# Top-k's copy to PSUM on VectorE instead of ScalarE, and an earlier hand-over of the low halves in U

## The chip, the cores and the metric

One core of a Trainium2 chip runs the whole program. Its engines are TensorE (PE in the profile, with its weight loads as PEld), VectorE (DVE), ScalarE (ACT), GpSimd (POOL) and SyncE (SP, which here only starts transfers). The metric is the device time of one execution in microseconds; lower is better.

## The reference

Two layers work on 272 rows (256 tokens and 16 meta rows) of width 1024. Each layer mixes tokens (a gated recurrence in layer 0, a convolution in layer 1), normalises, and then runs a feed-forward block that picks experts, which is where most of the time goes:

```python
q = (xc @ w_query).reshape(c, PEER_HEADS, 2, PEER_HALF)
scores = jnp.einsum('chpk,pnk->chpn', q, sub_keys.astype(q.dtype))
s1, i1 = lax.top_k(scores[:, :, 0], PEER_TOPK)
s2, i2 = lax.top_k(scores[:, :, 1], PEER_TOPK)
cand = (s1[..., :, None] + s2[..., None, :]).reshape(c, PEER_HEADS, PEER_TOPK * PEER_TOPK)
s, flat = lax.top_k(cand, PEER_TOPK)
...
expert = idx1 * PEER_N_KEYS + idx2
g = jax.nn.softmax(s.astype(jnp.float32), axis=-1).astype(xc.dtype)
act = jax.nn.gelu(jnp.einsum('chkd,cd->chk', expert_u[expert], xc))
return jnp.einsum('chk,chkd->cd', g * act, expert_v[expert])
```

There are 8 heads, 128 keys on each of two axes (so 16384 experts), and 16 experts are kept per row and head.

## The kernel before

The expert block is done mostly densely. For each of 128 tiles of 128 experts the kernel multiplies the tile of `peer_u` with all rows ("U", PE), applies gelu, multiplies with a gate matrix that is zero where an expert was not picked, and multiplies the result with the tile of `peer_v` ("V"). The last rows of a layer are left out of the dense work; for groups of 16 of them ("few") the picked rows of `peer_u` and `peer_v` are fetched by index (GpSimd's indirect transfers, `few_rows`), and DVE makes the dots (`few_mult`, L1147) and the weighted row sums (`few_add`, L1172 and L1174).

`linears` (from L192) runs over the tiles of U. `load_split` fetches a tile `raw` on SP's queue, ACT casts it to `hi` (L161), and DVE or GpSimd takes the low half `lo = raw - hi` (L170). PE then runs three times 8 matmuls for a tile (L198): hi with the high part of x, hi with the low part, lo with the high part. `raw` has four to five buffers, `hi` and `lo` two each in U. `u_store` (L633) is called behind each tile of U's first half (tiles 0 to 63): it sets the gelu on ACT (L656, `act_a`) and strews the other work between the tiles, by tile numbers at the top of the file. Who makes the low half is decided by `LO_FROM`: GpSimd for the tiles before it, DVE from it on.

Before U, PE makes the scores, ACT copies them out of PSUM (L619), and DVE picks the best: `topk_steps` (from L967). For one group of 128 rows this is 16 times five instructions over 128 scores (L976 to L980), then the copy of the second axis' values to PSUM (`pairs`, L985, on ACT), the sums of candidates (L990), eight times five instructions over the 112 candidates (L999 to L1003), the addresses (L1011 to L1022), and the one-hot look-up of the indices (L1030, L1036, L1041). The second group of rows (`c0` > 0) is done first and whole; the first group (`slow`) runs up to L1003 before U's low halves come to DVE, and its eight last steps are taken at the tiles listed in `SLOW`. In layer 0 one group of few rows needs a small top-k of its own (`few_topk`), whose candidate sums (L990, 128x64 and 128x48) read two tiles in SBUF.

The indices of the first finished group go through DRAM to the few rows: `few_spread` at tile `SPREAD`, `few_fetch` four tiles on, both on SP's queue, and `few_ids` on DVE makes addresses of them at tile `LO_FROM` + 1. Near the end of U's first half the softmax of each group (L1054 to L1065, with a tanh on ACT, L1055) and its turn (`topk_out`: three transposes on PE, L1225, copies on ACT, L1229 and L1230, and one subtraction on DVE) are placed at fixed tiles.

The scheduler keeps the program's order on each engine except where `issue_after` pins an instruction behind another, or where it moves one ahead of work that it does not depend on. Each engine takes its instructions in order.

Of the kernel before, what the change touches and what calls it, by code (L numbers as in the profile page):

```python
# [12 lines left out]
AF = mybir.ActivationFunctionType  # L13
# [21 lines left out]
FEW = META  # L35
DENSE_U, DENSE_V = (240, 224), (192, 176)
EARLY, DRAWN = ((240, 256), (240, 224)), ((224, 208, 192), (208, 192, 176))
DOTS_FROM, DOTS, ROWS, AHEAD, LO_FROM = 34, 20, 2, 2, 31
SLOW = (31, 32, 33, 34, 36, 38, 40, 42)
NEAR = 4  # L40
JG = 4
JA = 64
SPREAD = 26
WROW = 256
PIECES = (0, 32, 64, 96, 120, 128)
FULL = (("v", 1024),)
# [20 lines left out]
class Trunk:  # L67
# [514 lines left out]
    def peer(self, layer, n, xs):  # L582
        tc, nc, a = self.tc, self.nc, self.a
# [9 lines left out]
        with tc.tile_pool(name=f"few{layer}", bufs=1) as kp:  # L593
            iT = ip.tile([HK, n // HC, 2, HC, 2], F16, name="iT")
            ghT = ip.tile([HK, n, 2], F16, name="ghT")
            glT = ip.tile([HK, n], F32, name="glT")
            act_a = ap0.tile([P, JA, nu], F32, name="act_a")

            with tc.tile_pool(name=f"top{layer}", bufs=1) as sp:
                q = sp.tile([P, 2 * HEADS, nq], F32, name="q")  # L600
                for b, (t, bias) in enumerate(self.pre_q):
                    nc.scalar.activation(q[:, b, :], t, AF.Identity, bias=bias)
                self.linears([a["w_query"][layer, b] for b in range(2, 2 * HEADS)], xs, nq, FULL,
                             lambda b, ps: nc.vector.tensor_copy(q[:, 2 + b, :], ps), defer=2,
                             ring=(0, 1, 2, 7, 6))
                picked = []
                early, drawn = ([self.few_new(kp, layer, t0) for t0 in g[layer]] for g in (EARLY, DRAWN))
                near = [few for few in early + drawn if few["t0"] < 2 * P]
                dots = [(few, 0, k) for few in early for k in range(TOPK)]
                dots, later = dots[:DOTS], dots[DOTS:]  # L610
                for c0, md in ctiles:
                    sc = sp.tile([P, 2 * HEADS, NK], F32, tag="sc", name="sc", bufs=2)
                    for g in range(4):
                        ps = self.psum("sps", (3, 4)).rearrange("p (a b) -> p a b", a=4)
                        for i in range(4):
                            b = 4 * g + i
                            nc.tensor.matmul(ps[:, i, :], q[:, b, c0:c0 + P], self.sk[:, 2 * layer + b % 2, :],
                                             start=True, stop=True)
                        nc.scalar.activation(sc[:, 4 * g:4 * g + 4, :], ps, AF.Copy)  # L619
                    if c0:  # L620
                        picked.append((c0, md, *self.topk(sp, sc, P, self.bank(7, "pairs"), True)))
                        for few in early:
                            self.few_turn(sp, few, xs)
                        for few in early:
                            if few not in near:
                                self.few_topk(sp, few, q)
                    else:
                        slow = self.topk_steps(sp, sc, P, HEADS, 2, self.bank(7, "pairs"))
                        for _ in range(3 * HEADS):
                            next(slow)  # L630
                        picked.append((c0, md))

                def u_store(j, ps):  # L633
                    self.fifth = True
                    if j in (LO_FROM, SLOW[-1]):
                        with tc.issue_after(self.last_load):
                            self.few_load(*((sp, early[0], "turned") if j == LO_FROM else (kp, early[1], "kept")))
                    behind = [few for few in early if few.get("left")]
                    if j in SLOW:
                        with tc.issue_after(self.dve_lo.ins):  # L640
                            try:
                                next(slow)
                            except StopIteration as end:
                                picked[-1] += end.value
                    elif j > SLOW[-1] and behind:
                        with tc.issue_after(self.dve_lo.ins):
                            for _ in range(min(2, behind[0]["left"])):
                                self.few_picked(behind[0])
                    e, step = divmod(3 * (j - DOTS_FROM), 4)
                    if 0 <= e < DOTS + AHEAD and step < 3:  # L650
                        with tc.issue_after(self.dve_lo.ins), tc.issue_after(self.lo_ins.ins):
                            if e >= AHEAD:
                                self.few_mult(dots[e - AHEAD][0], dots[e - AHEAD][2])
                            if e < DOTS:
                                self.few_rows(sp, *dots[e], AHEAD + 1)
                    last = nc.scalar.activation(act_a[:, j, :], ps, AF.Gelu_apprx_tanh)  # L656
                    i = j - (JA - 6 - 2 * len(picked))
                    t, odd = divmod(i, 2)
                    if 0 <= t < len(picked) and not odd:
                        c0, m, idx, fv = picked[t]  # L660
                        with tc.issue_after(last.ins), tc.issue_after(self.dve_lo.ins):
                            picked[t] = c0, m, idx, self.softmax(sp, fv, P)
                    if j == SPREAD:
                        with tc.issue_after(self.last_load):
                            self.few_spread(nc.sync, near, "pos", picked[0][2])
                    if j == JA - 1:
                        with tc.issue_after(self.last_load):
                            self.few_spread(nc.sync, near, "z", picked[0][3][:, None])
                    if j == SPREAD + 4:
                        with tc.issue_after(self.last_load):  # L670
                            self.few_fetch(nc.sync, near, "pos")
                    at = 0 if j == LO_FROM + 1 else j - SLOW[-1] - 3
                    if j == LO_FROM + 1 or 0 < at < len(near):
                        with tc.issue_after(self.dve_lo.ins):
                            self.few_ids(near[at], near[at]["pos"])
                    if t == len(picked) and not odd:
                        with tc.issue_after(last.ins):
                            for few in early:
                                if few not in near:
                                    self.few_soft(sp, few)  # L680
                    if 0 < t <= len(picked) and not odd:
                        with tc.issue_after(last.ins), tc.issue_after(self.mm.ins):
                            self.topk_out(*picked[t - 1], iT, ghT, glT)
                self.linears([U[j] for j in range(JA)], xs, nu, lambda j: FULL if j >= LO_FROM else (("p", 1024),), u_store)

            with tc.tile_pool(name=f"act1{layer}", bufs=1) as ap1:
# [104 lines left out]
                for e, (few, i, k) in enumerate(ops):  # L791
                    t = e * (NK - JA - 7) // len(ops) + (2 if i and few is second_ else 0)
# [174 lines left out]
    def topk_steps(self, sp, sc, m, H, parts=1, ps=None, beside=False):  # L967
        nc = self.nc
        K = TOPK
        sv = sp.tile([P, H, 2, K], F32, tag=f"sv{H}", name="sv", bufs=1)  # L970
        si = sp.tile([P, H, 2, K], U32, tag=f"si{H}", name="si", bufs=1)
        for b in range(2 * H):
            s = sc[:m, b, :]
            v, i = sv[:m, b // 2, b % 2, :], si[:m, b // 2, b % 2, :]
# [7 lines left out]
        sv1 = sv[:m, :, 1]  # L982
        if ps is not None:
            sv1 = ps[:m, :H * K].rearrange("p (h k) -> p h k", h=H)
            nc.scalar.activation(sv1, sv[:m, :, 1], AF.Copy)  # L985
        cand = sp.tile([P, H, NEAR * K + (K - NEAR) * NEAR], F32, tag=f"cand{H}", name="cand", bufs=1)
        for part, rows, cols in ((cand[:m, :, :NEAR * K], slice(0, NEAR), slice(0, K)),
                                 (cand[:m, :, NEAR * K:], slice(NEAR, K), slice(0, NEAR))):
# [6 lines left out]
        for h in range(H):  # L995
            s = cand[:m, h]
            v, i = fv[:m, h, :], fi[:m, h, :]
# [502 lines left out]
```

## Time and profile before

| | |
|---|---|
| median of 3 runs | 1816.5 us (1814.68 to 1819.98) |
| the profiled execution | 1818.11 us |
| its span, first to last instruction | 1816.3 us |
| mean granted TensorE clock | 0.972 |
| lo (L170): DVE, GpSimd | 492 at 1225 ns, 62 at 2390 ns |
| hi (L161), ACT | 554 at 1059 ns |
| GpSimd's mean for an indirect row load of `peer_u`, `peer_v` | 1341 ns, 1756 ns |

The page gives for each engine its busy time, a row of 40 slices of the span, and groups of equal instructions with their mean; the list of waits says who stood idle in front of which line and what ended it; a timeline gives instructions in order of time, with the idle time before each in brackets. A group on one line can hold several shapes.

### The profile page before, as it was taken

How to read it: one execution, taken by the hardware profiler on the slowest of the kernel's cores; microseconds unless marked ns; L12 is line 12 of the kernel's file. 1: busy time of each engine (PE TensorE's matmuls, PEld its weight loads, DVE VectorE, ACT ScalarE, POOL GpSimd, SP SyncE). 2: the span in 40 equal slices, each digit the busy share in tenths (PEclk: the TensorE clock that was granted, in tenths of full speed). 3: DMA queues.
4: the chain of work that ended last, by engine and by line, in shares of the span. 5: the costliest groups of instructions: out<-in, count | busy, mean ns of one | idle time of the engine just before them, and what ended most of it. 6: DMA issues, size and time to landing. Idle time of an engine off the chain costs nothing. (4 is left out here: it accounts for less than half of the span.)

```text
span 1816.3 us, 35341 instructions
## 1 busy us (share of the span) xinstructions
PE 1704.8 (94%) x13420; PEld 1661.3 (91%) x13420; DVE 1483.7 (82%) x2888; ACT 1000.8 (55%) x1862; POOL 716.0 (39%) x492
## 2 busy tenths in 40 slices
PE   8999389999999999999999993899999999999997
PEld 7899389999999999999989893899999999999997
DVE  7786933989999789998789869338799997899886
ACT  5553144457777555787532541444577765555453
POOL 1101276324454567753000012763243335687520
PEclk9999699999999999999999996899999999999999
DMA  5545257978788899999541462479797888999984
GB/s 198 163 154 150 58 163 247 343 255 290 252 267 271 303 331 361 369 376 330 198 140 47 133 193 58 151 246 332 257 296 267 278 267 319 348 374 370 338 324 166
DMA packets 136059, 453.35 MB, mean 250 GB/s; under 512 B 23632, under 2 KB 24784, under 8 KB 135760
## 3 DMA queue, kind: packets, MB, share of 16 engines
q1 hardware_dynamic: 98256, 326.23, 53.3%
q0 software_dynamic: 37632, 124.85, 19.0%
q8 instruction: 105, 1.72, 0.4%
q14 instruction: 66, 0.54, 0.1%
HBM read 438.15 MB, written 12.87 MB: 248 GB/s over the span
## 5 line engine op out<-in xcount | busy, mean ns | idle before, releaser
L161 ACT ACTIVATE hi<-raw 128x1024 fp32r<-128x1024 f32 x554 | 586.1, 1059 | 519.3 <-PE acc L820 194.4
L170 DVE TENSOR_TENSOR lo<-raw,hi 128x1024 fp32r<-128x1024 f32 x492 | 600.9, 1225 | 213.6 <-ACT hi L161 198.7
L198 PE MATMUL u<-xs,hi 128*128 128x224 f32 (+3 forms) x4544 | 577.6, 279 | 78.1 <-ACT hi L161 77.3
L198 PEld LDWEIGHTS u<-xs,hi 128*128 128x128 f32 x4544 | 546.1, 193 | 80.5 <-ACT hi L161 78.9
L820 PE MATMUL acc<-w,hi 128*128 128x384 f32 (+1 forms) x1952 | 377.7, 335 | 0.0
L1141 POOL DMA_INDIRECT rows<-peer_v,ids x160 | 280.9, 1756 | 240.3 <-DVE few_out L1174 111.3
L820 PEld LDWEIGHTS acc<-w,hi 128*128 128x128 f32 x1952 | 322.9, 190 | 0.0
L198 PE MATMUL u<-xs,lo 128*128 128x224 f32 (+3 forms) x2272 | 308.4, 277 | 1.3 <-DVE lo L170 1.3
L198 PEld LDWEIGHTS u<-xs,lo 128*128 128x128 f32 x2272 | 282.4, 191 | 1.9 <-DVE lo L170 1.9
L824 PE MATMUL acc<-w,lo 128*128 128x192 f32 (+1 forms) x2016 | 264.2, 272 | 6.4 <-DVE turn L1150 4.6
L824 PEld LDWEIGHTS acc<-w,lo 128*128 128x128 f32 x2016 | 260.2, 192 | 9.3 <-DVE lo L170 9.1
L170 POOL TENSOR_TENSOR lo<-raw,hi 128x1024 fp32r<-128x1024 f32 x62 | 148.0, 2390 | 197.1 <-ACT hi L161 122.2
L1174 DVE SCALAR_TENSOR_TENSOR few_out<-rows,act,few_out 128x1024 f32<-128x1024 f32 x150 | 193.1, 1287 | 20.4 <-DMA rows<-peer_v,ids 17.3
L1141 POOL DMA_INDIRECT rows<-u_rows,ids x64 | 85.8, 1341 | 201.2 <-DVE rows L1147 146.9
L1151 POOL DMA_INDIRECT act<-own,turn x96 | 125.7, 1310 | 31.6 <-issue 24.7
L715 ACT ACTIVATE Bl<-AB,glT 128x128 f16<-128x128 f16 x368 | 112.7, 389 | 21.6 <-PE g L731 16.5
L245 PE MATMUL u<-x,raw 128*128 128x272 f32 x480 | 114.7, 399 | 5.2 <-DMA x<-h 5.2
L245 PEld LDWEIGHTS u<-x,raw 128*128 128x128 f32 x480 | 92.9, 194 | 24.7 <-DMA raw<-w_in 5.1
L1147 DVE SCALAR_TENSOR_TENSOR rows<-rows,wide 128x1024 f32<-128x1024 f32 x64 | 78.0, 1219 | 4.7 <-DMA rows<-u_rows,ids 4.7
L409 POOL TENSOR_SCALAR xs<-x,par 128x272 fp32r<-128x272 f32 (+1 forms) x4 | 3.5, 882 | 180.2 <-DVE x L395 180.2
L710 DVE TENSOR_TENSOR AB<-iota,iT 128x2048 f16<-128x2048 f16 x46 | 57.1, 1245 | 0.0
L985 ACT ACTIVATE pairs<-sv 128x128 f32<-128x128 f32 x4 | 1.1, 281 | 89.7 <-DVE sv L979 89.7
(313 smaller groups left out, 1763.4 us busy)
## 6 DMA issues: line engine op xcount, KB each, us to landing
raw<-peer_u SPq DMA_DIRECT2D x256, 512.0 KB
raw<-peer_v SPq DMA_DIRECT2D x248, 512.0 KB
raw<-w_query SPq DMA_DIRECT2D x28, 512.0 KB
raw<-pw SPq DMA_DIRECT2D x22, 512.0 KB
raw<-w_in SPq DMA_DIRECT2D x16, 512.0 KB
own<-own POOLq DMA_DIRECT2D x18, 256.0 KB
raw<-w_out SPq DMA_DIRECT2D x8, 512.0 KB
raw<-peer_v SPq DMA_DIRECT2D x16, 256.0 KB
```

Source lines behind the costliest of these rows:

```text
L161: self.act_hi = nc.scalar.activation(hi, raw, AF.Copy).ins
L170: i = e.tensor_tensor(lo[:, s], raw[:, s], hi[:, s].bitcast(F32), op=OP.subtract)
L198: self.mm = nc.tensor.matmul(ps[:, :n], l[:, k, :], xs(k, r)[:, :n], start=start, stop=stop)
L245: self.mm = self.nc.tensor.matmul(ps[:, :n], raw[:, k, :], x[:, k, :n], start=k == 0, stop=k == NB - 1)
L710: nc.vector.tensor_tensor(AB.rearrange("p x c (a b) -> p (x c) a b", b=2), keys, iT[:, c0 // HC].rearrange("p x c b -> p (x c) b")[:, :, N ...
L715: nc.scalar.activation(Bl[:, c], Bh[:, c], AF.Copy, scale=glT[:, c0 + c:c0 + c + 1])
L820: self.mm = nc.tensor.matmul(acc[b][:, :2 * n].rearrange("p (a t) -> p a t", a=2), hi, w[:, :, :n], start=j == 0, stop=j == NK - JG - 1, s ...
L824: self.mm = nc.tensor.matmul(main[b][:, :n], hi if p_ else lo, w[:, i, :n], start=False, stop=j == NK - 1 and not p_, skip_group_check=True)
L1141: self.last_rows = self.nc.gpsimd.indirect_dma_start(out=t, out_offset=None, in_=table, in_offset=bass.IndirectOffsetOnAxis(ap=few["ids"][ ...
L1147: self.nc.vector.scalar_tensor_tensor(t, t, 1.0, few["x"], op0=OP.mult, op1=OP.mult, accum_out=few["act"][:, k:k + 1])
L1151: self.nc.gpsimd.indirect_dma_start(out=few["act"][:, k:k + 1], out_offset=None, in_=few["table"].rearrange("p j (t o) -> (p j t) o", o=1) ...
L1174: nc.vector.scalar_tensor_tensor(few["out"], t, w, few["out"], op0=OP.mult, op1=OP.add)
```

## The change

The copy to PSUM in `topk_steps` is made by DVE. `LO_FROM` goes from 31 to 27, and the steps of the slow top-k (`SLOW`) and the first dot (`DOTS_FROM`) come four tiles earlier with it. U's first half does 23 dots in place of 20. Of the second few group 5 row sums in place of 2 are made in U's second half, and so three fewer are left for V. The indices are spread at tile 24, not 26. The first softmax is placed at tile 50 and turned at 53 (before: 54 and 56); the second is placed at 54 and turned at 58 (before: 56 and 58).

```diff
-DOTS_FROM, DOTS, ROWS, AHEAD, LO_FROM = 34, 20, 2, 2, 31
-SLOW = (31, 32, 33, 34, 36, 38, 40, 42)
+DOTS_FROM, DOTS, ROWS, AHEAD, LO_FROM = 30, 23, 5, 2, 27
+SLOW = (27, 28, 29, 30, 32, 34, 36, 38)
+SOFT, OUT = {50: 0, 54: 1}, {53: 0, 58: 1}
...
-SPREAD = 26
+SPREAD = 24
...
-                    i = j - (JA - 6 - 2 * len(picked))
-                    t, odd = divmod(i, 2)
-                    if 0 <= t < len(picked) and not odd:
+                    if j in SOFT:
+                        t = SOFT[j]
...
-                    if t == len(picked) and not odd:
+                    if j == max(OUT):
...
-                    if 0 < t <= len(picked) and not odd:
+                    if j in OUT:
                         with tc.issue_after(last.ins), tc.issue_after(self.mm.ins):
-                            self.topk_out(*picked[t - 1], iT, ghT, glT)
+                            self.topk_out(*picked[OUT[j]], iT, ghT, glT)
...
-            nc.scalar.activation(sv1, sv[:m, :, 1], AF.Copy)
+            nc.vector.tensor_copy(sv1, sv[:m, :, 1])
```

Lines of the changed kernel between the new table and `u_store` stand one further down (hi is L162 there, lo L171). The first place is ACT at the start of U in layer 0; `sc` are the scores, `turned` the few rows for the dots, `act_a` a tile's gelu. Before:

```order
L985 ACTIVATE pairs<-sv 128x128
L161 ACTIVATE hi<-raw 128x1024
L1089 ACTIVATE turned<-wide_ps 16x512 x2
L656 ACT_TABLE_LOAD
L656 ACTIVATE act_a<-u 128x240
L161 ACTIVATE hi<-raw 128x1024
L656 ACTIVATE act_a<-u 128x240
L161 ACTIVATE hi<-raw 128x1024
L656 ACTIVATE act_a<-u 128x240
L161 ACTIVATE hi<-raw 128x1024
L656 ACTIVATE act_a<-u 128x240
L985 ACTIVATE pairs<-sv 128x128
```

The same place in the changed kernel:

```order
L620 ACTIVATE sc<-sps 128x512 x4
L162 ACTIVATE hi<-raw 128x1024
L1089 ACTIVATE turned<-wide_ps 16x512 x2
L657 ACT_TABLE_LOAD
L657 ACTIVATE act_a<-u 128x240
L162 ACTIVATE hi<-raw 128x1024
L657 ACTIVATE act_a<-u 128x240
```

Both copies have left ACT's queue, with hi and act_a in the same order as before; on DVE each now stands one or two instructions ahead of the candidate sums (L990).

The second place is GpSimd, from the low halves of U's first half to the second half in layer 0; `rows` are row loads of the few groups. Before:

```order
L170 TENSOR_TENSOR lo<-raw,hi 128x1024 x31
L1141 DMA rows<-u_rows,ids_1618 128x1024 x16
L1141 DMA rows<-u_rows,ids_1624 128x1024 x6
L773 COPY own<-act_a 128x512
L774 DMA own_224_4356<-own 128x512
```

Now:

```order
L171 TENSOR_TENSOR lo<-raw,hi 128x1024 x27
L1141 DMA rows<-u_rows,ids_1618 128x1024 x16
L1141 DMA rows<-u_rows,ids_1624 128x1024 x9
L773 COPY own<-act_a 128x512
L774 DMA own_224_4365<-own 128x512
```

Four low halves have gone to DVE, and three more row loads of the second group stand ahead of the first `own`.

The third place is ACT near the end of U's first half in layer 0, from the tanh of the second softmax (`z`, 128x128) to the copies of its turn (`iT`, `ghT` with 256 columns). Before:

```order
L1055 ACTIVATE z<-z 128x128
L1229 ACTIVATE iT<-tps 128x8x16 x2
L1230 ACTIVATE ghT<-tps 128x128
L161 ACTIVATE hi<-raw 128x1024
L656 ACTIVATE act_a<-u 128x240
L161 ACTIVATE hi<-raw 128x1024
L656 ACTIVATE act_a<-u 128x240
L1055 ACTIVATE z<-z 128x16
L1229 ACTIVATE iT<-tps 128x16x16 x2
L1230 ACTIVATE ghT<-tps 128x256
```

Now:

```order
L1055 ACTIVATE z<-z 128x128
L162 ACTIVATE hi<-raw 128x1024
L657 ACTIVATE act_a<-u 128x240
L162 ACTIVATE hi<-raw 128x1024
L657 ACTIVATE act_a<-u 128x240
L162 ACTIVATE hi<-raw 128x1024
L657 ACTIVATE act_a<-u 128x240
L162 ACTIVATE hi<-raw 128x1024
L657 ACTIVATE act_a<-u 128x240
L1055 ACTIVATE z<-z 128x16
L1229 ACTIVATE iT<-tps 128x16x16 x2
L1230 ACTIVATE ghT<-tps 128x256
```

Between softmax and turn there were two tiles and the first group's turn; now there are four tiles, and the first turn lies further ahead.

## The prediction

> **What bounds the kernel now.** The page comes first: busy shares and the 40 slices (45.4 us each).
>
> ```profile
> PE 1704.8 (94%) x13420; PEld 1661.3 (91%) x13420; DVE 1483.7 (82%) x2888; ACT 1000.8 (55%) x1862; POOL 716.0 (39%) x492
> PE   8999389999999999999999993899999999999997
> PEclk9999699999999999999999996899999999999999
> ```
>
> TensorE (PE) works 94% of the span. It has two holes, slices 4 and 24 (busy 3 tenths), and its granted clock falls only there (6, and 6 and 8). Both lie at the start of a U stage, one per layer. The list of waits names what ended them:
>
> ```profile
> ACT pairs L985 <- DVE sv L979: 89.7, 4, 37.0
> PE u L198 <- ACT hi L161: 77.3, 7, 33.4
> ```
>
> ScalarE (ACT) waited 89.7 us in four waits in front of the copy to PSUM (L985), and PE waited 77.3 us for the cast hi (L161). The timeline of layer 0 shows that one causes the other. First ACT, then PE (the bracket is the idle time before a row and what ended it):
>
> ```profile
> 183.78 0.28 ACT L985 ACTIVATE pairs<-sv 128x128 f32<-128x128 f32 x1 [9.64 <-DVE sv L979]
> 183.99 1.04 ACT L161 ACTIVATE hi<-raw 128x1024 fp32r<-128x1024 f32 x1
> ...
> 231.24 0.28 ACT L985 ACTIVATE pairs<-sv 128x128 f32<-128x128 f32 x1 [37.02 <-DVE sv L979]
> 231.45 1.04 ACT L161 ACTIVATE hi<-raw 128x1024 fp32r<-128x1024 f32 x1
> ```
>
> ```profile
> 173.26 2.03 PE L198 MATMUL u<-xs,hi 128*128 128x240 f32 x16
> 176.03 1.95 PE L198 MATMUL u<-xs,hi 128*128 128x240 f32 x16
> ...
> 185.08 3.77 PE L198 MATMUL u<-xs,hi 128*128 128x240 f32 x16 [6.21 <-ACT hi L161]
> ...
> 232.55 3.57 PE L198 MATMUL u<-xs,hi 128*128 128x240 f32 x16 [33.45 <-ACT hi L161]
> 236.85 1.95 PE L198 MATMUL u<-xs,hi 128*128 128x240 f32 x16
> 238.63 1.07 PE L198 MATMUL u<-xs,lo 128*128 128x240 f32 x8
> 239.53 1.96 PE L198 MATMUL u<-xs,hi 128*128 128x240 f32 x16
> ```
>
> Each row of 16 with hi begins a tile, so U tile 0 starts at 173.26, tile 1 at 176.03, tile 2 at 185.08, tile 6 at 232.55, tile 7 at 236.85. ACT takes its instructions in order. The copy waits until VectorE (DVE) has its 16 pairs of top-k steps, and the cast of the next tile stands behind it. After each hole PE's first 16 matmuls take 3.57 to 3.77 us, not 1.95. Undisturbed, a tile takes 2.68 us (236.85 to 239.53). Layer 1 is the same:
>
> ```profile
> 1087.64 2.03 PE L198 MATMUL u<-xs,hi 128*128 128x224 f32 x16
> ...
> 1090.40 1.95 PE L198 MATMUL u<-xs,hi 128*128 128x224 f32 x16
> ...
> 1099.84 3.76 PE L198 MATMUL u<-xs,hi 128*128 128x224 f32 x16 [6.60 <-ACT hi L161]
> ...
> 1143.29 3.75 PE L198 MATMUL u<-xs,hi 128*128 128x224 f32 x16 [29.48 <-ACT hi L161]
> ...
> 1147.87 1.95 PE L198 MATMUL u<-xs,hi 128*128 128x224 f32 x16
> ```
>
> **The change part by part.** *The copy on DVE.* DVE made the data, so the copy waits for nothing there. A copy to PSUM with twice the elements is the cast L1011 (row below, 416 ns); 0.2 to 0.4 us each, 0.6 us for two, on DVE's chain alone. On ACT, hi of tile 2 stands behind scores and turned rows only, and PE goes on with tile 2 behind tile 1. Tile 7 then starts in layer 0 at 176.03 + 6 × 2.68 = 192.1 and not 236.85: 44.7 us. In layer 1 it starts at 1090.40 + 6 × 2.68 = 1106.5 and not 1147.87: 41.4 us. Together 86.1 us, all on PE's path, the slow-clock tiles included.
>
> Can the others follow at 2.68 us a tile? GpSimd (POOL) makes the low halves of tiles 0 to 26 now:
>
> ```profile
> 194.04 2.40 POOL L170 TENSOR_TENSOR lo<-raw,hi 128x1024 fp32r<-128x1024 f32 x1 [0.63 <-ACT hi L161]
> 240.02 2.41 POOL L170 TENSOR_TENSOR lo<-raw,hi 128x1024 fp32r<-128x1024 f32 x1 [0.29 <-ACT hi L161]
> ```
>
> 2.40 us beside a busy DVE and 2.41 beside a nearly idle one: it fits, with a gap of 0.29 us.
>
> *The low halves from tile 27.* This moves the hand-over from POOL to DVE four tiles forward. In tiles DVE has 27 instead of 31, in time far less: its top-k used to have PE's holes as cover, and they go. DVE's last top-k instructions, and what it did next:
>
> ```profile
> 242.59 0.27 DVE L1003 FIND_INDEX8 fi<-fv,r 128x8 uint32<-128x112 f32 x1
> 299.15 1.23 DVE L170 TENSOR_TENSOR lo<-raw,hi 128x1024 fp32r<-128x1024 f32 x1 [56.30 <-ACT hi L161]
> ...
> 1153.33 0.27 DVE L1003 FIND_INDEX8 fi<-fv,r 128x8 uint32<-128x112 f32 x1
> ```
>
> DVE was done at 242.9 and 1153.6 and then idle for 56.3 us. Tile 27 will start at 176.03 + 26 × 2.68 = 245.7 (layer 1: 1160.1); PE uses its low half 1.78 us later (236.85 to 238.63), and DVE needs 1.23 us to make it. So DVE must be free by 246.3 (1160.6): slack 3.4 and 7.0 us. Against that stands a new collision. In the old holes POOL was idle; now it is busy 2.4 of every 2.68 us:
>
> ```profile
> 195.47 1.05 DVE L990 TENSOR_TENSOR cand<-sv 128x64 f32<-128x64 f32 x1
> ...
> 196.69 0.20 DVE L990 TENSOR_TENSOR cand<-sv 128x48 f32<-128x48 f32 x1
> ...
> 197.66 0.20 DVE L1016 TENSOR_SCALAR far<-fi 128x128 uint32<-128x128 uint32 x1
> ...
> 198.39 0.28 DVE L1021 SCALAR_TENSOR_TENSOR pu<-pu,fi 128x128 uint32<-128x128 uint32 x1
> ```
>
> The 64-wide sum took 1.05 us and ended as POOL's lo of 194.04 ended (196.44); the 48-wide one behind it took 0.20. That is 0.85 us of waiting for POOL. The six address steps from 197.66 to 198.39 ran with POOL idle. Now two sums (layer 0 only) and six steps meet a busy POOL. Bounds: nothing, if all fall into gaps; a whole lo for each, 8 × 2.40 = 19 us and 6 × 2.40 = 14 us. I take half a lo for the first of a bunch, and two or three short steps per gap (they start 0.13 us apart), which is nearest to the one blocked row: the sums 2, the six steps 1.2 + 2 × 2.68 = 6.6, less 1 for their own run: 7 us in layer 0 and 5.5 in layer 1. PE then waits 7 + 0.6 − 3.4 = 4 us in layer 0 (bounds 0 and 16) and 0 in layer 1 (0 and 8).
>
> The Trainium skill, "SBUF — State Buffer", section "Who interferes with whom", says that a VectorE instruction in a 2-port mode or with two SBUF inputs and a GpSimd one that reads SBUF exclude each other for a whole instruction. The row of 1.05 us agrees. By that rule every one of the eight can be blocked, which is the upper bound above; the sum goes by the rows.
>
> The long one-hot steps have one operand in PSUM; the nearest row is the cast to PSUM, which ran unhurt beside POOL's lo in the stretch from 185 to 199 us:
>
> ```profile
> L1011 DVE CAST pairs<-si 128x256 f32<-128x256 uint32 x1 | 0.4, 416 | 0.0
> ```
>
> I cost them at nothing here.
>
> *23 dots and 5 row sums.* Three dots per layer move from U's second half into its first, and three row sums from V into U's second half.
>
> ```profile
> L1174 DVE SCALAR_TENSOR_TENSOR few_out<-rows,act,few_out 128x1024 f32<-128x1024 f32 x150 | 193.1, 1287 | 20.4 <-DMA rows<-peer_v,ids 17.3
> ...
> L1147 DVE SCALAR_TENSOR_TENSOR rows<-rows,wide 128x1024 f32<-128x1024 f32 x64 | 78.0, 1219 | 4.7 <-DMA rows<-u_rows,ids 4.7
> ...
> 300.00:345.00 45.00, 45.00 (x403) 45.00 (x403) 41.93 (x83) 22.34 (x34) 14.81 (x11) 1.00 0.88 315
> 585.00:930.00 345.00, 342.92 (x2359) 336.19 (x2358) 291.63 (x372) 221.02 (x351) 166.75 (x132) 1.00 0.86 311
> ```
>
> (The last two are stretches: length, then busy time of PE, weight loads, DVE, ACT, POOL.) The first half keeps its density: three dots in four tiles behind the hand-over, as in 300 to 345, where PE was busy 45.00 of 45 us with DVE at 41.93. The second half trades 3 × 1.22 for 3 × 1.29 us: nothing. V loses 3.9 us of DVE work per layer where PE is idle for 2.1 of 345 us: 0, at most 2 per layer. Each of these brings its row load on POOL's queue, one for one. On SP's queue the index transfers stand two loads earlier, while their reader on DVE (ids, behind tile 28's low half) comes four tiles earlier, near 249. SP comes to the last of them when load 28 finds a buffer, that is after the low half of tile 23, which starts at 176.03 + 22 × 2.68 = 235. I cost this at nothing, since some 13 us lie between; if the indices were late, DVE would stand in front of them with the low half of tile 29 queued behind.
>
> *First softmax sooner, turns later.* The second transposes waited for DVE's softmax in both layers:
>
> ```profile
> 379.96 0.33 PE L1225 MATMUL tps<-ident,z 128*128 128x128 f32 x1 [1.97 <-DVE z L1065]
> ...
> 1290.50 0.48 PE L1225 MATMUL tps<-ident,z 128*128 128x128 f32 x1 [1.97 <-DVE z L1065]
> 1290.63 3.57 PE L198 MATMUL u<-xs,hi 128*128 128x224 f32 x16
> ...
> 1294.93 1.95 PE L198 MATMUL u<-xs,hi 128*128 128x224 f32 x16
> ```
>
> Now four tiles lie between softmax and turn instead of two, 5.4 us more: both waits go (2 × 1.97), and layer 1's slow tile behind it (1294.93 − 1290.63 = 4.30, not 2.68: 1.6). Together 5.6; at least 0, if the next wait is as long.
>
> The sum: 86.1 + 5.6 − 4 = 87.7 us. The profiled execution took 1818.1 us (its span 1816.3 and 1.8 around it): 1730.4. The median of the runs is 1.6 lower: 1728.8, so **1729 us**.
>
> **The rivals.** (1) *DVE hands over late.* Each of the eight steps waits a whole lo, in both layers: 24 us of waiting instead of 4, 1749 us. For it: the row of 1.05 us, and a slack of only 3.4. Against: 0.85 us is all that was lost in four lo's.
>
> (2) *ACT stops at the next thing.* The second turned rows need the buffer of the first, and so the first's transfer, which now has less time for it; a table load follows, and both stand ahead of hi of tile 3. If a wait there were as long as the first hole (6.2 us and about 2 more for its slow clock, 8 a layer), the time would be 1745. The profile shows no wait at that place, but the transfer always had the copy's wait as cover.
>
> (3) *Slower than before.* If the ordinary top-k instructions (max, find, replace) were also shut out by POOL. Some 300 of them per layer now run beside POOL; if one in ten waited a lo, 30 × 2.68 = 80 us, less the 44.7 + 3.4 that are there to lose, 32 a layer: 1816.5 + 64 = 1880. It decides from 18 blocked instructions a layer on. Against it stands the group of finds from 185 to 199 us, beside four lo's, with a mean of 276 ns where the last one of 242.59, with POOL between two lo's, took 0.27:
>
> ```profile
> L1000 DVE FIND_INDEX8 fi<-fv,cand 128x8 uint32<-128x112 f32 x9 | 2.5, 276 | 0.0
> ```
>
> (4) *Nothing moves*, because hi waits for something else than the copy: 1816. The rows 183.78 and 183.99 speak against it.
>
> **How the numbers follow.** Forecast 0.82, (1) 0.10, (2) 0.05, (3) 0.02, (4) 0.01. The forecast's own range: no collision and 2 us from V per layer, 1721; to half of the upper bounds, 1737. With most of (1) and all of (2): 1721 to 1746. About 0.3% is what a measurement of this kernel can tell from no change; faster by more 0.97, within it 0.01, slower 0.02.
>
> **What would show it.** No row pairs on ACT; PE without a wait for hi near 179 and 200; tile 7 near 192; clock 9 in slices 4 and 24. POOL busy nine tenths from tile 2 to 26. DVE's sums and address steps longer than 0.2 to 0.3 us, ended with POOL's lo; in layer 0 a PE wait of some 4 us for DVE's lo near 250, in layer 1 none. No wait above 1 us before the second transposes. It is wrong if U still has holes over 10 us, or if DVE's lo makes PE wait beyond tile 32.

## The result, and the profile after

The changed kernel takes 1715.46 us, the median of six runs (1714.68 to 1719.34), where the kernel before took 1817.84 (six runs, 1814.68 to 1820.09). The ratio is 0.944, with a 95% interval of 0.9426 to 0.9455. The forecast was 1729 with a range from 1721 to 1746: the direction and the main mechanism, the copy, hold, but 102.4 us were gained where the sum had 87.7, and the time lies below the range.

The page of the changed kernel, the same three lines as before:

```profile
PE 1687.2 (98%) x13420; PEld 1647.0 (96%) x13420; DVE 1498.9 (87%) x2900; ACT 1000.1 (58%) x1858; POOL 685.3 (40%) x484
PE   8999999999999999999999999999999999999997
PEclk9999999999999999999999999999999999999999
```

TensorE (PE) works 98% of the span, both holes are gone, and the granted clock no longer falls in any slice. The start of U in layer 0, on PE, is a tile every 2.69 us from the second on:

```profile
172.85 2.05 PE L199 MATMUL u<-xs,hi 128*128 128x240 f32 x16
...
175.64 1.96 PE L199 MATMUL u<-xs,hi 128*128 128x240 f32 x16
...
178.33 1.96 PE L199 MATMUL u<-xs,hi 128*128 128x240 f32 x16
```

The hand-over of the low halves at tile 27 is the one wait that the prediction placed in U's first half of layer 0. It is there, and shorter than the 4 us foreseen:

```profile
245.66 1.95 PE L199 MATMUL u<-xs,hi 128*128 128x240 f32 x16
248.86 1.17 PE L199 MATMUL u<-xs,lo 128*128 128x240 f32 x8 [1.25 <-DVE lo L171]
```

To see where the 102.6 us of span went (1816.3 to 1713.7), the start of the same matmul is set side by side in the two traces; the last column is how far the changed kernel is ahead there.

| start on PE of | before | after | ahead |
|---|---|---|---|
| U tile 0, layer 0 | 173.26 | 172.85 | 0.41 |
| U tile 7 | 236.85 | 191.80 | 45.05 |
| U tile 26 | 287.95 | 242.97 | 44.98 |
| U tile 28 | 293.33 | 249.87 | 43.46 |
| U tile 56 | 368.65 | 326.06 | 42.59 |
| U's second half (first g) | 402.62 | 356.98 | 45.64 |
| V (first acc) | 592.49 | 544.31 | 48.18 |
| U tile 0, layer 1 | 1087.64 | 1039.82 | 47.82 |
| U tile 7 | 1147.87 | 1058.66 | 89.21 |
| U tile 28 | 1204.15 | 1114.94 | 89.21 |
| U tile 56 | 1279.19 | 1190.83 | 88.36 |
| U's second half | 1314.67 | 1221.62 | 93.05 |
| V | 1499.79 | 1406.11 | 93.68 |
| end of V (first row L1421) | 1797.02 | 1694.39 | 102.63 |

The first half of U gives 45.2 us in each layer (45.64 − 0.41 and 93.05 − 47.82). That is near the forecast. What the prediction left at nothing is the last line: V of layer 1 gives 8.95 us, while V of layer 0 with the work behind it gives nothing (48.18 to 47.82). The second halves give 2.5 and 0.6.

In the trace of before, V of layer 1 has a place that the prediction never showed. On PE:

```profile
1690.45 2.01 PE L824 MATMUL acc<-w,lo 128*128 128x176 f32 x8 [3.50 <-DVE turn L1150]
1692.26 2.62 PE L820 MATMUL acc<-w,hi 128*128 128x352 f32 x8
1694.67 1.84 PE L824 MATMUL acc<-w,lo 128*128 128x176 f32 x8
...
1698.66 1.50 PE L820 MATMUL acc<-w,hi 128*128 128x352 f32 x8
1700.00 1.02 PE L824 MATMUL acc<-w,lo 128*128 128x176 f32 x8
```

PE waited 3.50 us, and the matmuls behind the wait ran slowly: 2.01, 2.62 and 1.84 us, where 1.02, 1.50 and 1.02 are usual, some 2.9 more. The releaser named is a tiny copy on VectorE (DVE), but it only stood last in a line. DVE, and the queue of GpSimd (POOL), at the same time:

```profile
1687.92 1.28 DVE L1174 SCALAR_TENSOR_TENSOR few_out<-rows,act,few_out 128x1024 f32<-128x1024 f32 x1 [4.36 <-DMA rows<-peer_v,ids]
1689.12 0.15 DVE L1150 COPY turn<-ids 128x1 uint32<-128x1 uint32 x1
1689.18 1.22 DVE L170 TENSOR_TENSOR lo<-raw,hi 128x1024 fp32r<-128x1024 f32 x1
```

```profile
1674.69 2.04 POOL L1151 DMA_INDIRECT act<-own,turn  x1 [0.30 <-issue]
1677.03 1.83 POOL L1151 DMA_INDIRECT act<-own,turn  x1 [0.30 <-issue]
1679.16 1.68 POOL L1141 DMA_INDIRECT rows<-peer_v,ids  x1 [0.30 <-DVE w L293]
```

DVE stood 4.36 us before a row sum, with the low half that PE wanted queued behind. Counted from the end of V, where each load meets its sum one for one, the row that it waited for was loaded by the issue of 1679.16, which stood behind two gathers of activations (draws) and landed 8.76 us after it began. The two draws held the queue from 1674.69 on, 4.47 us, about as long as DVE then waited.

### The profile page after: what moved, and what is told of

The parts are those of the page before. It is cut to its first block, busy times and chain, and to the rows that moved or that the text cites. A ratio compares the mean times of both kernels' runs of the same rounds, so it can differ in the third digit from the quotient of the medians.

```text
span 1713.7 us, 35354 instructions
## 1 busy us (share of the span) xinstructions
PE 1687.2 (98%) x13420; PEld 1647.0 (96%) x13420; DVE 1498.9 (87%) x2900; ACT 1000.1 (58%) x1858; POOL 685.3 (40%) x484
## 4 chain that ended last, share of the span: by engine, by line
PE 86%; DVE 10%; ACT 2%; issue 1%; DMA 1%; DVEq 0%; SPq 0%; ACTq 0%
PE u L199 41%; PE acc L820 19%; PE acc L824 13%; PE u L246 6%; PE cv L1374 2%; PE g L730 1%; PE g L731 1%; PE acc L866 1%; DVE lo L171 1%; ACT hi L162 1%; DVE si L980 1%; DVE r L978 1%; PE var L956 1%; DVE si L977 1%; PE pre L266 0%
## 5 line engine op out<-in xcount | busy, mean ns | idle before, releaser
L162 ACT ACTIVATE hi<-raw 128x1024 fp32r<-128x1024 f32 x554 | 586.1, 1059 | 517.1 <-PE acc L820 197.4
L171 DVE TENSOR_TENSOR lo<-raw,hi 128x1024 fp32r<-128x1024 f32 x500 | 612.8, 1229 | 112.4 <-ACT hi L162 98.5
L199 PE MATMUL u<-xs,hi 128*128 128x224 f32 (+3 forms) x4544 | 568.2, 276 | 2.5 <-ACT hi L162 1.9
L199 PEld LDWEIGHTS u<-xs,hi 128*128 128x128 f32 x4544 | 537.0, 190 | 4.0 <-ACT hi L162 2.6
L1141 POOL DMA_INDIRECT rows<-peer_v,ids x160 | 275.8, 1724 | 280.2 <-DVE few_out L1174 151.1
L171 POOL TENSOR_TENSOR lo<-raw,hi 128x1024 fp32r<-128x1024 f32 x54 | 129.3, 2399 | 108.4 <-PE u L199 72.0
L1141 POOL DMA_INDIRECT rows<-u_rows,ids x64 | 89.6, 1400 | 189.3 <-DVE rows L1147 140.8
L1151 POOL DMA_INDIRECT act<-own,turn x96 | 120.6, 1256 | 35.0 <-issue 23.5
L730 PE MATMUL g<-AB 128*128 128x128 f16 x368 | 46.5, 220 | 0.0
```

Source lines behind the costliest of these rows:

```text
L162: self.act_hi = nc.scalar.activation(hi, raw, AF.Copy).ins
L171: i = e.tensor_tensor(lo[:, s], raw[:, s], hi[:, s].bitcast(F32), op=OP.subtract)
L199: self.mm = nc.tensor.matmul(ps[:, :n], l[:, k, :], xs(k, r)[:, :n], start=start, stop=stop)
L730: nc.tensor.matmul(ps[:, c, :], A, Bh, start=True, stop=False)
L1141: self.last_rows = self.nc.gpsimd.indirect_dma_start(out=t, out_offset=None, in_=table, in_offset=bass.IndirectOffsetOnAxis(ap=few["ids"][ ...
L1151: self.nc.gpsimd.indirect_dma_start(out=few["act"][:, k:k + 1], out_offset=None, in_=few["table"].rearrange("p j (t o) -> (p j t) o", o=1) ...
```

## The experiments

Theory A: what the gain had beyond the sum is that late rows no longer stop DVE in V of layer 1, because three row loads fewer stand in POOL's queue there. Rival B: those waits depend on how the streams fall, and go with any shift in time. All ratios are to runs of the kernel before.

**The copy alone.**

```
-            nc.scalar.activation(sv1, sv[:m, :, 1], AF.Copy)
+            nc.vector.tensor_copy(sv1, sv[:m, :, 1])
```

> The kernel before with one line changed: the copy to PSUM on VectorE. All theories: tile 7 of U starts near 192 in layer 0 (236.85 before), and some 86 us of holes go. Theory A (what the change gained beyond the sum is the load waits in V of layer 1, and they go because three row sums leave each V): V still has all its row sums here, so those waits stay, about 9 us with the slow clock behind them: 1817.8 - 86 = 1732 us, ratio 0.953, and the trace shows a TensorE wait of 1 to 4 us near 1600. Rival B (those waits depend on how the streams happen to fall, and any shift of 86 us can remove them): 1722 to 1732, no such wait needed. VectorE's last top-k instruction of layer 0 ends near 247.7 as in the changed kernel, with the hand-over at tile 31 four tiles later, so TensorE does not wait for a low half near 249. The 1.97 us waits before the second transposes stay.

Measured, with this line alone changed in the kernel before: 1730.27 us (1726.54 to 1734.69), ratio 0.9519 (0.9498 to 0.9539). That is near A's 1732 but still within B's 1722 to 1732, so here the trace has to tell them apart. U tile 7 of layer 0 starts at 192.49, DVE's last top-k instruction ends at 248.35 and no low half is waited for near 249. The waits before the second transposes are 1.96 and 1.97 us as before. V of layer 1 still has its waits, the longest of them:

```profile
1603.36 1.13 PE L824 MATMUL acc<-w,lo 128*128 128x176 f32 x8 [2.41 <-DVE lo L170]
```

**All but the copy.** The same line the other way round in the changed kernel.

> The changed kernel with the copy back on ScalarE, all else as changed. The holes come back: 33.4 and 29.5 us, tile 7 near 236.5. Theory A: what is left is turns (5.6) and V with fewer row sums (about 9, and 2 in layer 0): 1817.8 - 16 = 1802 us, ratio 0.991. Rival B: only the turns are left, 1812 us, ratio 0.997. Rival C (the parts other than the copy cost something by themselves, because the hand-over at tile 27 comes right behind the holes, where VectorE is still busy): above 1812. VectorE ended its top-k at 242.9 before; tile 27 comes at 290, so no wait for a low half is expected there.

Measured: 1800.94 us (1798.35 to 1805.79), ratio 0.9905 (0.9885 to 0.9924): A's 1802, and neither B's 1812 nor C's loss. The holes are back:

```profile
184.46 3.77 PE L199 MATMUL u<-xs,hi 128*128 128x240 f32 x16 [6.19 <-ACT hi L162]
231.66 3.77 PE L199 MATMUL u<-xs,hi 128*128 128x240 f32 x16 [33.46 <-ACT hi L162]
```

The copy alone is worth 87.4 us and the rest alone 16.7: together 104, about the 102.4 of the whole. The parts add up.

**The row sums back in V.**

```
-DOTS_FROM, DOTS, ROWS, AHEAD, LO_FROM = 30, 23, 5, 2, 27
+DOTS_FROM, DOTS, ROWS, AHEAD, LO_FROM = 30, 20, 2, 2, 27
```

> The changed kernel with 20 dots and 2 row sums as before, so that each V has its three row sums again. Theory A: V of layer 1 gets its load waits back: 1715.5 + 9 = 1724.5, up to 1727 with layer 0, ratio 0.949, and the trace has TensorE waits of together 3 us or more in V of layer 1 behind a VectorE that waits for rows. Rival B: 1715.5 within 2, and no such waits.

Measured: 1725.68 us (1724.29 to 1728.48), ratio 0.949 (0.9473 to 0.9508), 10 us more than the changed kernel, as A says. B falls: this kernel is shifted by the same 86 us and has the waits. V of layer 1 as a stretch (length; busy time of PE, weight loads, DVE, ACT, POOL; granted clock; DMA share; GB/s), and what DVE waited for in it, first of the kernel before, then of this one, then of the changed kernel:

```profile
1499.80:1797.00 297.20, 290.27 (x2102) 287.79 (x2100) 252.97 (x283) 156.42 (x163) 164.65 (x116) 0.99 0.93 337
DVE few_out L1174 <- DMA rows<-peer_v,ids: 10.7, 9, 4.4
```

```profile
1409.50:1707.30 297.80, 288.93 (x2102) 286.58 (x2101) 252.63 (x283) 156.35 (x163) 162.13 (x116) 0.99 0.92 337
DVE few_out L1174 <- DMA rows<-peer_v,ids: 13.1, 9, 3.5
```

```profile
1406.10:1694.40 288.30, 286.62 (x2103) 285.17 (x2102) 248.89 (x280) 156.11 (x163) 158.01 (x113) 1.00 0.94 342
DVE few_out L1174 <- DMA rows<-peer_v,ids: 4.7, 6, 1.4
```

With three loads fewer (62 to 59) the stretch is 9 us shorter, and DVE waits 4.7 us for rows in place of 10.7 or 13.1. In the three kernels with 2 row sums in U and all their work the stretch takes 294.8 to 297.8 us, and in the six with 5 it takes 287.5 to 288.4. So the row sums are worth 6 to 10 us there.

**The old places of softmax and turn.**

```
-SOFT, OUT = {50: 0, 54: 1}, {53: 0, 58: 1}
+SOFT, OUT = {54: 0, 56: 1}, {56: 0, 58: 1}
```

> The changed kernel with the softmaxes and turns in the old places (54 and 56, 56 and 58). The sum's term for them was 5.6 us; in the trace of the changed kernel the same stretch is 2.2 us shorter in layer 0 and 3.9 in layer 1. So 1715.5 + 6 = 1721.5, ratio 0.9475, with TensorE waits of about 2 us before the second transposes. Rival: the waits before the transposes came from holes and not from the places, and the time stays at 1715.5.

Measured: 1718.92 us (1715.40 to 1719.47), ratio 0.945 (0.9432 to 0.9468): 3.5 us more in the median, less than the 6 expected, and the intervals overlap. The trace shows why it is less:

```profile
335.58 0.33 PE L1225 MATMUL tps<-ident,z 128*128 128x128 f32 x1 [0.99 <-DVE z L1065]
...
1200.80 0.33 PE L1225 MATMUL tps<-ident,z 128*128 128x128 f32 x1 [1.07 <-DVE z L1065]
```

The old places cost 1 us of waiting each, not 1.97, beside the other edits. From U tile 28 to the second half this kernel takes 0.9 and 1.2 us more than the changed one, where the kernel before took 2.2 and 3.8 more. The rest of that came with the other edits, and two traces narrow it down. With the copy alone the stretch takes 109.4 and 110.6 us, no less than before (109.3 and 110.5). With the dots and row sums put back, and the other edits kept, it takes 107.1 and 106.7, as in the changed kernel. What is left, the slow steps and index transfers that come earlier, was not tried by itself.

**What in V is short: loads, sums or POOL's queue?** Three kernels that start from the one with 2 row sums. First a third of the loads out:

```
+                if k and (s - ahead) % 3 == 2:
+                    few["rows"][k] = self.held
+                self.held = few["rows"][k]
                 self.few_add(few, k, *few["home"])
...
-            if s < len(rows):
+            if s < len(rows) and not (rows[s][1] and s % 3 == 2):
```

> The kernel of the run before with 2 row sums and 20 dots (1725.7 us, V of layer 1 with about 9 us of TensorE waits), and in V every third row load left out: its sum takes the row loaded before it again, so that part of the output is of other rows. 62 sums stay on VectorE per layer, some 42 loads are left on GpSimd's queue and on the DMA engines. If the loads (queue and transfer) are what V of layer 1 waits for: the waits go, 1725.7 - 9 = 1716.5, ratio 0.944, VectorE waits under 3 us for rows. If VectorE's own work is what is short: 1725.7 within 2.

Measured: 1714.78 us (1713.79 to 1716.18), ratio 0.9432 (0.9412 to 0.9452). All 62 sums are there and all but 0.4 us of PE's waits in V of layer 1 are gone, so DVE's own work isn't what is short.

Then a third of the sums out:

```
+                if k and (s - ahead) % 3 == 2:
+                    few["rows"].pop(k)
+                else:
+                    self.few_add(few, k, *few["home"])
```

> The same kernel with all loads, but every third sum left out, so that those rows don't count in the output: some 20 x 1.28 = 26 us less of VectorE's work in each V, GpSimd's queue and the DMA engines as full as before. If VectorE's work is what is short: 1716 or below. If the loads are: 1725.7 within 3, with VectorE's waits for rows of 10 us or more in V of layer 1.

Measured: 1787.20 us (1782.81 to 1787.96), ratio 0.9827 (0.9804 to 0.9849), far above both expectations. The experiment brought a wait of its own, on POOL in V of layer 1:

```profile
POOL rows L1141 <- DMA rows<-peer_v,ids: 98.4, 19, 9.1
```

Together with the edit this row says that a load that overwrites a row which nobody read waits in POOL's queue until the load before it in that buffer has landed, up to 9.1 us each, and everything behind stands. (The trace doesn't name the buffer; that it is the same one is argued from the edit.) So it can't tell what DVE's work costs; it does show what a blocked POOL queue does to V (324.1 us for the stretch).

Then half of the draws out:

```
+        if k % 2:
+            self.nc.vector.memset(few["act"][:, k:k + 1], 0.0)
+            return
         self.nc.gpsimd.indirect_dma_start(
```

> The same kernel with every second gather of activations (draw) replaced by a zero, so that those rows get no weight: 24 fewer gathers of 1.26 us and 0.30 us of issue each, 37 us of GpSimd's queue in each V, while the 512 KB row loads stay. If GpSimd's queue is what makes the row loads late (a load stands behind two draws, up to 4.4 us): 1716.5. If the transfers themselves are late, with the DMA engines 0.92 to 0.94 busy: 1725.7 within 2.

Measured: 1717.45 us (1714.83 to 1718.08), ratio 0.9446 (0.9426 to 0.9466). The same stretch, V of layer 1, and DVE's waits for rows in it (the sums stand on L1177 here):

```profile
1406.60:1693.80 287.20, 286.42 (x2103) 285.05 (x2102) 252.84 (x307) 156.31 (x163) 133.47 (x92) 1.00 0.94 349
DVE few_out L1177 <- DMA rows<-peer_v,ids: 3.1, 7, 1.0
```

All 62 row loads are there, the DMA engines are as full as in the changed kernel (0.94, at 349 GB/s), and yet the waits went with 24 small gathers. It is the place in POOL's queue that makes the rows late, not the bytes. The small gathers' own packets are no rival: the packets of POOL's DMA queue took 29.6% of the DMA engines' time here and 30.0% with all 48 gathers (1409 to 1700 in both traces). Whether a load loses its time among POOL's instructions or in that DMA queue behind them, the run can't tell apart.

**How far it can be pushed.** Eight row sums in the second half of U (below); then 5 row sums but 20 dots (30, 20, 5, 2, 27); then 6 with 24 dots (29, 24, 6, 2, 27). The second half has 33, 33 and 30 steps, where both kernels have 30.

```
-DOTS_FROM, DOTS, ROWS, AHEAD, LO_FROM = 30, 23, 5, 2, 27
+DOTS_FROM, DOTS, ROWS, AHEAD, LO_FROM = 30, 23, 8, 2, 27
```

> The changed kernel with 8 row sums in the second half of U in place of 5. V loses three more: at most the 1.1 us of waits that are left in V of layer 1. The second half of U takes 33 steps of 1.28 us where it had 30: VectorE is busy 162.7 of 169 us there, 166.6 would be left nearly no gap. As the prediction argued (VectorE's work there costs nothing): 1714.5. If the second half of U is full: 1715.5 + 1 to 4 us, with TensorE waits for low halves or for AB there.

> The changed kernel with 20 dots, as before, and 5 row sums, as changed: the second half of U takes 33 steps where both kernels had 30, V is as in the changed kernel. If the second half has room (as the prediction costed it): 1715.5. If it is full, as the run with 8 row sums says (8.4 us longer in layer 1, 1.8 in layer 0): 1724, ratio 0.949; then the three dots moved forward are what made room for the three row sums.

> The changed kernel with one more dot in the first half of U (24, from tile 29) and one more row sum in the second (6): the second half keeps its 30 steps, V loses one more load per layer. If V of layer 1 is short of load time and each load out of it is worth about 3 us until the waits (1.1 us of TensorE) are gone: 1714.4. Rival: dots from tile 29 stand too close behind the indices, or the second half is disturbed: 1717 or above.

Measured: 1724.38 us (1721.21 to 1731.54; ratio 0.9495, 0.9468 to 0.9521), 1726.02 (1723.04 to 1729.37; 0.9492, 0.9465 to 0.9518) and 1714.00 (1713.27 to 1717.30; 0.9429, 0.9404 to 0.9454). The second half of U in both layers, of the changed kernel and of the one with 20 dots:

```profile
357.00:544.30 187.30, 187.30 (x1850) 186.56 (x1849) 180.06 (x257) 145.45 (x394) 75.05 (x51) 1.00 0.82 272
1221.60:1406.10 184.50, 184.50 (x1818) 184.01 (x1817) 175.52 (x249) 139.00 (x376) 67.73 (x51) 1.00 0.83 277
```

```profile
356.80:550.90 194.10, 189.43 (x1850) 187.30 (x1849) 184.25 (x263) 145.47 (x394) 86.13 (x54) 1.00 0.82 270
1230.40:1417.20 186.80, 185.37 (x1819) 184.42 (x1819) 178.17 (x255) 139.67 (x376) 68.22 (x54) 1.00 0.85 282
```

In the changed kernel, with 30 steps, PE is busy in every microsecond of it; with 33 the two stretches are 9.1 us longer. Six sums with 24 dots shorten V of layer 1 to 286.7 us, but the time can't be told from that of the changed kernel.

**The price of the collision.** The six address steps (L1016 to L1021) of the wide top-k written twice:

```
+        for _ in range(2 if beside else 1):
-        nc.vector.tensor_scalar(far, fp, cut, cut, op0=OP.max, op1=OP.subtract)
+            nc.vector.tensor_scalar(far, fp, cut, cut, op0=OP.max, op1=OP.subtract)
...
```

> The changed kernel with the six address steps (L1016 to L1021) of the wide top-k written twice, the second time with the same results. In the trace of the changed kernel the six took 4.6 us beside GpSimd's low halves in layer 0 (two of them blocked, 1.56 and 2.49 us). If blocked steps wait for the gap behind a low half and the ones behind them use the same gap: two more periods of 2.68, 5.4 us in each layer; layer 0 hands over 5.4 later (TensorE wait near 249 of 6 to 7 us in place of 1.25, and 1 to 2 us of slow clock), layer 1 has 2.8 us of slack, so 2.6 more: 1715.5 + 5.4 + 1.5 + 2.6 = 1725. If every step waits a whole low half (the prediction's upper bound): 12 x 2.7 = 32 us of steps, 1745. If they are hardly blocked, 6 x 0.13 = 0.8 us, one layer: 1716.

Measured: 1727.55 us (1726.94 to 1728.08), ratio 0.9498 (0.9474 to 0.9522): 12.1 more, of which U's first half has 9.6 (7.45 in layer 0, 2.18 in layer 1, by the starts as in the table) and the rest comes behind it. First the DVE rows of the second six, then POOL's low halves at that time, then PE's wait:

```profile
203.09 2.44 DVE L1017 TENSOR_SCALAR far<-fi 128x128 uint32<-128x128 uint32 x1
205.44 0.21 DVE L1018 TENSOR_SCALAR pu<-fi 128x128 uint32<-128x128 uint32 x1
...
206.05 2.48 DVE L1022 SCALAR_TENSOR_TENSOR pu<-pu,fi 128x128 uint32<-128x128 uint32 x1
```

```profile
203.04 2.40 POOL L171 TENSOR_TENSOR lo<-raw,hi 128x1024 fp32r<-128x1024 f32 x1 [0.24 <-ACT hi L162]
205.92 4.91 POOL L171 TENSOR_TENSOR lo<-raw,hi 128x1024 fp32r<-128x1024 f32 x2 [0.48 <-ACT act_a L657]
```

```profile
254.20 2.06 PE L199 MATMUL u<-xs,lo 128*128 128x240 f32 x8 [6.60 <-DVE lo L171]
```

The second six took 203.09 to 208.53, 5.4 us: two periods of a tile, with two blocked steps, and four that ran in gaps. That is the middle case. A step that starts inside a low half ends with it, and what follows it runs free in the gap. The upper bound of the prediction, a whole low half for each step, is refuted.

**The hand-over one tile later.**

```
-DOTS_FROM, DOTS, ROWS, AHEAD, LO_FROM = 30, 23, 5, 2, 27
-SLOW = (27, 28, 29, 30, 32, 34, 36, 38)
+DOTS_FROM, DOTS, ROWS, AHEAD, LO_FROM = 31, 23, 5, 2, 28
+SLOW = (28, 29, 30, 31, 33, 35, 37, 39)
...
-SPREAD = 24
+SPREAD = 25
```

> The changed kernel with the hand-over one tile later: low halves on VectorE from tile 28, its slow steps, dots and index transfers one tile later too. VectorE ended its top-k at 247.7 in layer 0; the low half of tile 28 is wanted 2.7 us later than that of tile 27, so the 1.25 us wait goes and the 1.57 us that the tile lost with it: 1714, and no TensorE wait for a low half near 250. Rival: the later steps make the second transposes wait again (up to 2 us a layer): 1717 or above.

Measured: 1713.03 us (1712.15 to 1717.59), ratio 0.9423 (0.9397 to 0.9449). PE has no wait at tiles 27 and 28:

```profile
247.14 1.06 PE L199 MATMUL u<-xs,lo 128*128 128x240 f32 x8
248.04 1.96 PE L199 MATMUL u<-xs,hi 128*128 128x240 f32 x16
249.84 1.06 PE L199 MATMUL u<-xs,lo 128*128 128x240 f32 x8
```

The median is the lowest of all, 2.4 us below the changed kernel, as the trace leads one to expect (1.5), but the intervals overlap.

## Why the prediction was right, and where it was wrong

**The copy: right to the tenth.** Tile 7 started at 191.80 (192.1 foretold) and 1058.66. From tile 0 to tile 7 layer 0 gained 45.05 − 0.41 = 44.6 us (44.7) and layer 1 89.21 − 47.82 = 41.4 (41.4). The copy takes 0.27 us on DVE (0.2 to 0.4). Rivals (2) to (4) fall with the same rows: no wait for the next thing on ACT, no blocked max, find or replace (means of 0.26 to 0.29 us beside POOL), and the holes did hang on the copy.

**The collision: the mechanism right, the size too large.** DVE in layer 0 of the changed kernel:

```profile
195.27 2.18 DVE L990 TENSOR_TENSOR cand<-sv 128x64 f32<-128x64 f32 x1
...
198.60 1.56 DVE L1016 TENSOR_SCALAR far<-fi 128x128 uint32<-128x128 uint32 x1
...
200.49 2.49 DVE L1020 TENSOR_TENSOR pu<-pu,far 128x128 uint32<-128x128 uint32 x1
...
247.42 0.27 DVE L1003 FIND_INDEX8 fi<-fv,r 128x8 uint32<-128x112 f32 x1
247.60 1.21 DVE L171 TENSOR_TENSOR lo<-raw,hi 128x1024 fp32r<-128x1024 f32 x1
```

Three of the eight steps were blocked. Beyond what they cost before (1.05, 0.20 and, free of POOL, 0.28) they lost 1.1, 1.4 and 2.2 us: 4.7, where 7 had been put. So DVE came to the low half of tile 27 at 247.60 and not near 250, PE waited 1.25, and two tiles lost 44.98 − 43.46 = 1.5 us and not 4; rival (1), a whole low half for each step, is out. In layer 1 two steps were blocked (0.44 and 2.48 us), and DVE then stood idle for 1.20 us before the hand-over: nothing lost, as foretold. The Trainium skill, "SBUF — State Buffer", section "Who interferes with whom", says that the one that comes first holds the shared port for its whole instruction; the rows of 2.44 and 2.48 us (six steps written twice) and 2.49 us (changed kernel), of three kinds of operation, agree.

**Softmax and turns: the size right, the cause only in part.** 45.64 − 43.46 = 2.2 in layer 0 and 93.05 − 89.21 = 3.8 in layer 1, 6.0 together (5.6). The second transposes no longer wait:

```profile
334.36 0.27 PE L1225 MATMUL tps<-ident,z 128*128 128x128 f32 x1
...
1199.09 0.27 PE L1225 MATMUL tps<-ident,z 128*128 128x128 f32 x1
```

But with the old places put back beside the other edits only 0.9 + 1.2 = 2.1 us returned. The other 3.9 came with edits that the prediction had not counted here, so that the term came out is in good part luck. By tile 56 each layer is 0.9 us behind, because the first turn's transposes now stand ahead of that tile (with a wait of 0.2 to 0.3 us for a cast behind them); more than that is won later.

**23 dots and 5 row sums: the step that failed.** The prediction put "V loses 3.9 us of DVE work per layer where PE is idle for 2.1 of 345 us: 0, at most 2 per layer". Measured were 8.95 us in V of layer 1, and the kernels that differ in the row sums put their part of it at 6 to 10. Two things were wrong with the step. The stretch it was read from, 585 to 930, is V of layer 0, and it was taken for both layers; V of layer 1 had 6.9 us of idle PE (297.20 − 290.27) and slow matmuls behind the longest wait. V of layer 0 by itself, in the kernel before, had 0.8:

```profile
592.50:893.00 300.50, 299.70 (x2114) 298.48 (x2112) 258.36 (x289) 196.41 (x296) 163.12 (x126) 1.00 0.93 337
```

The sign stood in a row that the prediction itself quotes: the row sums waited 17.3 us for rows, of which 10.7 were in that one stretch. And the edit was priced as DVE's work alone, where what it takes out of V is three loads from POOL's queue. The prediction named these loads ("one for one") and gave them no price. The runs with a third of the loads and with half of the draws left out show that this queue is the cause.

The second halves of U, also put at nothing, gave 2.5 and 0.6 us, but not by the dots and row sums. With the copy alone they take 187.8 and 184.5 us (402.62 to 592.49 and 1314.67 to 1499.79 before, 189.9 and 185.1); with everything but the copy they take 190.0 and 185.9. So this gain came with the copy; why was not tried.

The sum with the measured terms is 44.6 + 41.4 of the copy, 1.5 less of the collision, 6.0 of the turns, 0.4 at the start, 3.2 in the second halves and 8.6 in V (8.95 − 0.36): 102.7, for 102.6 of span. Of the 15 us that the sum missed, 8.6 are V, most or all of it the row sums, 3.2 the second halves and 2.5 the collision. The range failed mainly by the same step, since its low end had "at most 2 per layer" from V. The "nothing" for the trade in the second half held only because the three dots left it at the same time: without that, 33 steps cost 9 us there.

## What to carry to other kernels

Read a stage's waits in every layer that runs it, before a part is priced at nothing: the same code had 1 us of waits in one layer and 7 in the other. A step that is moved takes its place in each in-order queue with it; where a queue of gathers runs close behind its readers, one load in twenty less can be worth more than the arithmetic that goes with it. Short instructions that can be blocked by another engine's don't each pay: of a bunch of six here two were blocked, and the others ran in the gaps behind them.

## What had not been expected of the hardware

A load into a buffer that nobody read in between held up the queue that issues it until the former load had landed (98.4 us in 19 waits in one V, read as above); whether the program's own ordering or the chip asks for that, no run shows. And matmuls can run slowly behind waits well under 3 us, or run at full speed behind a longer one. Four rows of PE in the kernel with a third of the sums out:

```profile
1598.02 1.13 PE L824 MATMUL acc<-w,lo 128*128 128x176 f32 x8 [2.90 <-DVE turn L1150]
1598.99 1.50 PE L820 MATMUL acc<-w,hi 128*128 128x352 f32 x8
...
1612.68 1.21 PE L824 MATMUL acc<-w,lo 128*128 128x176 f32 x8 [1.62 <-DVE lo L171]
1613.68 2.62 PE L820 MATMUL acc<-w,hi 128*128 128x352 f32 x8
```

After 2.90 us of waiting the next rows took 1.13 and 1.50 us, about the usual (granted clock 1.00 from 1596 to 1604); after 1.62 us they took 1.21 and 2.62 (0.72 from 1612 to 1618). The Trainium skill, "TensorE: Matmul & The Clock Gate", section "Part 1: The HAM clock gate", lets the clock fall after at least one idle window of some 3.4 us. The wait of 3.50 us with 2.01 and 2.62 us behind it agrees; the wait of 1.62 us differs and shows that less can be enough. So the length of the wait alone doesn't decide it, and what does was not tried.
